# Second feed-forward product of a fp32 streaming layer by seven block products in two of three token blocks, with other token blocks

## The chip, the cores and the metric

One core of a Trainium2 chip runs the whole program. The metric is the device time of that core for one execution, in microseconds; lower is better. The names of the engines: PE multiplies matrices, DVE and POOL work element by element, ACT applies functions and copies, SP issues the DMAs. PEld is the loading of weights into PE, which goes on beside the matmuls.

## The reference, cut to what matters

A layer with a convolution mixer and a banded attention mixer, a gated merge of the two, and a gated feed-forward part. It runs on 2048 prompt tokens and 64 sample tokens; all weights and data are float32. The width D is 1024, the hidden width of the feed-forward part is 2816 (22 rows of 128).

```
merged = jax.nn.sigmoid(g_conv) * conv_out + jax.nn.sigmoid(g_attn) * attn_out
x = x + gt1 * (merged @ p['w_o'])

h2 = rms_norm(x, p['norm2_g']) * (1 + sc2) + sh2
gate, up = jnp.split(h2 @ p['w_ffn_in'], 2, axis=-1)
x = x + gt2 * ((jax.nn.silu(gate) * up) @ p['w_ffn_out'])
```

The change concerns the last line: the product of the hidden values, tokens x 2816, with `w_ffn_out`, 2816 x 1024.

## The kernel before, in words

**Numbers.** Every float32 operand of a product is split into a high part and a low part (the value minus the high part), both of a type that PE takes at its faster rate. One product is then three matmuls into the same PSUM bank: high by high, high by low, low by high (`mm3`, L613). For data ACT writes the high part and DVE subtracts the low one; for weights ACT writes the high part and POOL or DVE the low one.

**Stages.** The projections and the mixers run first, over four blocks of tokens (`PBLOCKS`, L35). They end near 1250 to 1360 us and the diff doesn't touch them. Then come the blocks of `CBLOCKS` (L36): tokens 0 to 704, 704 to 1344, 1344 to 2112. For each block the kernel does the gated merge (`merge`, L1512), the product with `w_o` (`wo`, L1661), the residual with norm and transposed columns (`residual`, L1539), and then the feed-forward part.

**The first feed-forward product** already goes by seven products for eight (`up`, L1743). Tokens are split into two halves of the block, D into two halves, and gate and up columns of one row f take the place of the two columns of a 2x2 block matrix. A row costs 7 x 4 x 3 = 84 matmuls whose moving width is half a block. It runs through the 22 rows in order. Its partial sums lie in PSUM banks of the tag "y" (four banks) and for one of them "gp" (four banks); ACT and DVE turn them into the hidden value of the row: tanh on ACT (`tg`), the gate's product on DVE, the factor, then the high part on ACT and the low part on DVE (`hidden`, L1717). The second half's split is put off into the next row (`late`).

**The second feed-forward product** (`down`, L1794) is plain. Once for every two rows, between two steps of `up`, it takes the two rows' hidden values as stationary operands: for each tile of 128 tokens and each of two column halves of 512, two rows x three matmuls into a "gp" bank; then DVE adds the bank to the token tile's sum `acc` in SBUF (for the first two rows ACT copies). The last four rows are done after all of `up`: there DVE adds `acc`, multiplies by the gate `gt`, adds the residual `x`, and the result is stored.

**Weights.** The class `Weights` (L250) goes through the list that `weight_order` (L499) writes out. Raw weights land in staging buffers ("wst", "wup", "wfo"; `free_tag`, L322; `load`, L329); `split` (L395) makes a slab of high and low parts, of which five are held; `done` gives one back. The seven products of `up` need sums of weight columns, which POOL makes (`operand`, L364; buffers `ws`) and which are kept in DRAM as `sum_d`. Keys of the kinds in `KEPT` (L60), the rows of `w_ffn_out` ("fo") among them, are stored in DRAM as high and low parts in the first block and read back in the later ones. Which engine subtracts is chosen at L426.

**What sets the order.** Instructions of PE stand as the code calls them. Everything else passes the planner (`Stream`, L159, and `Lane`, L106): it keeps a cost model of each engine's load, and lets side work in (weight slabs, residual steps, stores) where it reckons an engine free. All engine instructions are recorded at one line of a wrapper (L101), so the profile tells them apart by tiles: `ps` and `pd` are banks of the first and the second product, `t..` and `b..` the columns' operands, `whi`/`wlo` slabs, `hid` the hidden value's parts.

```
if j == 0 and 2 <= f <= NF - 4:
    yield from (("fo", f - 2), ("fo", f - 1))
```

## Time and profile before

| what | value |
| --- | --- |
| runs, us | 3053.41, 3048.85, 3043.31 |
| median, us | 3048.85 |
| profiled execution, span | 3049.1 us (no other time of it is given) |
| instructions | 44460 |
| HBM read, written | 501.70 MB, 171.61 MB |

The profile is one execution. Its page gives for each engine the busy time and the share of the span; the chain of waits follows the last instruction back to what released each step; a view by stretches gives busy time between two times; a view of groups gives for each operation and tile its count, the busy time in us, the mean of one in ns, and the idle time of the engine before it with what ended that. In the timeline a row has its start, its length, the engine, the line, the operation and the tiles; "x2" is two of a kind in a run, and a bracket names a wait that ended just before. A start less an earlier start of the same kind, divided by the matmuls between, is the cadence at which PE issues.

### The profile page before, as it was taken

How to read it: one execution, taken by the hardware profiler on the slowest of the kernel's cores; microseconds unless marked ns; L12 is line 12 of the kernel's file. 1: busy time of each engine (PE TensorE's matmuls, PEld its weight loads, DVE VectorE, ACT ScalarE, POOL GpSimd, SP SyncE). 2: the span in 40 equal slices, each digit the busy share in tenths (PEclk: the TensorE clock that was granted, in tenths of full speed). 3: DMA queues.
4: the chain of work that ended last, by engine and by line, in shares of the span. 5: the costliest groups of instructions: out<-in, count | busy, mean ns of one | idle time of the engine just before them, and what ended most of it. 6: DMA issues, size and time to landing. Idle time of an engine off the chain costs nothing.

```text
span 3049.1 us, 44460 instructions
## 1 busy us (share of the span) xinstructions
PE 2959.9 (97%) x16403; PEld 2633.0 (86%) x16403; DVE 1783.9 (59%) x3435; ACT 1180.2 (39%) x2110; POOL 1031.4 (34%) x642
## 2 busy tenths in 40 slices
PE   7989898999999999998999999999999999999999
PEld 4789776888888788898999998989999999999998
DVE  5797687867977895454443436554444556343345
ACT  3324531453255257355334343443333244322321
POOL 0200210101011102348778774344445343333431
PEclk9999998999999999999999999999999999999999
DMA  9888788888987788866455469754444965334434
GB/s 343 265 276 293 230 289 264 280 259 264 306 281 245 248 267 284 262 231 232 167 182 182 147 207 333 243 166 152 152 152 138 347 209 194 125 114 131 139 112 161
DMA packets 480167, 676.27 MB, mean 222 GB/s; under 512 B 37716, under 2 KB 316104, under 8 KB 479949
## 3 DMA queue, kind: packets, MB, share of 16 engines
q1 hardware_dynamic: 467669, 656.04, 65.7%
q10 hardware_dynamic: 12280, 17.39, 1.6%
q8 instruction: 129, 2.11, 0.3%
q14 instruction: 89, 0.73, 0.1%
HBM read 501.70 MB, written 171.61 MB: 221 GB/s over the span
## 4 chain that ended last, share of the span: by engine, by line
PE 83%; DVE 8%; DMA 4%; POOL 2%; issue 1%; ACT 1%; SPq 0%; ACTq 0%; POOLq 0%; DVEq 0%
PE ps L101 52%; PE pd L101 17%; PE pw L101 6%; DVE y L101 3%; PE po L101 2%; PE sc L101 2%; PE ptp L101 2%; POOL r L101 1%; PE pt L101 1%; PE pa L101 1%; DVE pr L101 1%; POOL wlo L101 1%; DMA whi<-w_dfi_h 0%; DMA kk<-k_d 0%; DMA wst<-in_w_in 0%
## 5 line engine op out<-in xcount | busy, mean ns | idle before, releaser
L101 POOL TENSOR_TENSOR wlo<-wst,whi 128x1024 fp32r<-128x1024 f32 (+1 forms) x213 | 452.1, 2132 | 586.4 <-ACT whi L101 465.5
L101 PE MATMUL ps<-t,whi 128*128 128x352 f32 (+2 forms) x2112 | 509.7, 324 | 10.7 <-ACT t L101 5.7
L101 PE MATMUL pd<-whi,hid 128*128 128x512 f32 (+1 forms) x1496 | 466.0, 389 | 0.0
L101 ACT ACTIVATE whi<-wst 128x1024 fp32r<-128x1024 f32 (+1 forms) x270 | 260.3, 973 | 448.0 <-PE pd L101 179.2
L101 PE MATMUL ps<-b,whi 128*128 128x352 f32 (+2 forms) x1584 | 382.1, 325 | 2.7 <-ACT early L101 1.9
L101 PEld LDWEIGHTS ps<-t,whi 128*128 128x128 f32 x2112 | 370.5, 189 | 16.1 <-ACT t L101 7.1
L101 DVE SCALAR_TENSOR_TENSOR y<-u,wd,y 128x512 f32<-128x512 f32 (+1 forms) x480 | 368.3, 771 | 6.5
L101 PE MATMUL ps<-hh,whi 128*128 128x512 f32 (+2 forms) x992 | 363.9, 367 | 0.0
L101 PE MATMUL ps<-hl,whi 128*128 128x512 f32 (+2 forms) x992 | 346.8, 350 | 0.0
L101 PE MATMUL ps<-hh,wlo 128*128 128x512 f32 (+2 forms) x992 | 346.4, 349 | 0.0
L101 PE MATMUL ps<-t,wlo 128*128 128x352 f32 (+2 forms) x1056 | 341.4, 323 | 0.1
L101 PEld LDWEIGHTS pd<-whi,hid 128*128 128x128 f32 (+1 forms) x1496 | 276.1, 185 | 62.5
L101 DVE TENSOR_TENSOR acc<-acc,pd 128x512 f32<-128x512 f32 (+1 forms) x272 | 186.9, 687 | 207.7 <-PE pd L101 206.8
L101 PE MATMUL pd<-wlo,hid 128*128 128x512 f32 (+1 forms) x748 | 291.6, 390 | 0.0
L101 PEld LDWEIGHTS ps<-b,whi 128*128 128x128 f32 x1584 | 276.9, 188 | 4.5 <-ACT early L101 2.8
L101 PE MATMUL ps<-b,wlo 128*128 128x352 f32 (+2 forms) x792 | 256.5, 324 | 0.0
L101 POOL TENSOR_TENSOR r<-t,mhalf 128x8 f32<-128x8 f32 (+3 forms) x68 | 84.8, 1249 | 401.0 <-DVE t L101 377.7
L101 POOL TENSOR_TENSOR wlo<-wup,whi 128x1024 fp32r<-128x1024 f32 (+1 forms) x73 | 158.9, 2177 | 171.1 <-ACT whi L101 171.1
L101 PEld LDWEIGHTS ps<-hh,wlo 128*128 128x128 f32 x992 | 188.1, 190 | 22.5
L101 PEld LDWEIGHTS ps<-hh,whi 128*128 128x128 f32 x992 | 189.0, 190 | 18.6 <-issue 2.1
L101 PEld LDWEIGHTS ps<-hl,whi 128*128 128x128 f32 x992 | 189.0, 191 | 15.4 <-issue 1.7
L101 PEld LDWEIGHTS ps<-t,wlo 128*128 128x128 f32 x1056 | 199.9, 189 | 0.4 <-POOL wlo L101 0.4
(206 smaller groups left out, 5431.0 us busy)
## 6 DMA issues: line engine op xcount, KB each, us to landing
whi<-w_din_h SPq DMA_DIRECT2D x72, 512.0 KB, 6.0
wlo<-w_din_l SPq DMA_DIRECT2D x72, 512.0 KB, 6.8
wst<-sum_d SPq DMA_DIRECT2D x133, 256.0 KB, 3.0
wmod<-in_w_ada SPq DMA_DIRECT2D x48, 512.0 KB, 8.6
sum_d<-ws SPq DMA_DIRECT2D x88, 256.0 KB, 4.6
whi<-w_dfo_h SPq DMA_DIRECT2D x44, 512.0 KB, 5.4
wlo<-w_dfo_l SPq DMA_DIRECT2D x44, 512.0 KB, 6.0
wst<-in_w_ffn_in SPq DMA_DIRECT2D x83, 256.0 KB, 3.4
```

What stands on the lines that cost most here:

```text
L101: return f(*args, **kw)
```

## The change

Blocks become tokens 0 to 576, 576 to 1344 and 1344 to 2112. In the last two blocks (`s` is 1 or 2) rows 4 to 19 of the second product go in pairs (`PAIRS`), e and o, by seven products for eight. The left matrix has the two halves of the block's tokens (i = 0, 1) as its rows and the hidden rows e and o as its columns; the right one has w rows e and o as its rows and the two halves of the 1024 columns as its columns. With A11, A21 the two halves of row e, and A12, A22 those of row o, DVE makes S3 = A11 - A21, S2 = A22 - S3, S1 = S2 + A11, S4 = A12 - S2 and each is split into high and low parts (`paired`, `put`). With B11, B12 the column halves of weight row e and B21, B22 those of row o, POOL makes T3 = B22 - B12, T1 = B12 - B11, T2 = B22 - T1, T4 = B21 - T2 in the second block (`down_parts`); the slabs are stored and read back in the third.

The seven products come in four slabs (`DN`) at four places of the next pair's `up` (`dn_at`): B21 and T3 before the s1 step of the even row, T4 and B11 before its a22 step, T2 and T1, then B22, in the odd row (for the last pair B22 after all of `up`). Each product is three groups of three matmuls of 512 columns, one for every 128 tokens of a half. T4 goes on in the banks of T3, and T2, T1 and B22 in those of B11 (`CHAIN`); after each product DVE adds the bank as it then stands to one of the four quarters of `acc` (`INTO`), so that a bank is read between two of its partial sums. Only rows 20 and 21 are left for the last stage of these blocks. Before the first block's third and fourth row and for all its rows `down` stays as it was; rows 4 to 19 are not stored there any more, and their raw rows are loaded again in the second block (items "fr").

Further: where the planner's POOL load is more than 4 us ahead of PE's (`BEHIND`), the low parts of weights go to DVE; `tile_chunks` rounds up; buffers "t2" and "tg1" go from two to three; `hid` has eight slots of half a block in each of these blocks.

```
-CBLOCKS = [(0, 704), (704, 1344), (1344, 2112)]
+CBLOCKS = [(0, 576), (576, 1344), (1344, 2112)]
-KEPT = ("qkv", "in", "fi", "fo")
+KEPT = ("qkv", "in", "fi", "fo", "dn")
+PAIRS = range(4, NF - 2, 2)
+DN = (("B21", "T3"), ("T4", "B11"), ("T2", "T1"), ("B22",))
+BEHIND = 4000.0
...
-    t, n = tiles[len(tiles) // 2 - 1]
+    t, n = tiles[(len(tiles) + 1) // 2 - 1]
...
+        if name == "pool" and self.sum_pool and self.stream.load["pool"] - self.stream.load["pe"] > BEHIND:
+            e, name = self.dve, "dve"
...
+        elif key[0] == "dn":
+            parts = [(slice(j, j + 1), part) for j, part in enumerate(self.down_parts(key))]
             self.stream.after("act", "pool")
...
+def dn_at(f):
+    return (0, 1, 3, 6 if f == PAIRS[-1] else 4)
...
-                if j == 0 and 2 <= f <= NF - 4:
+                if s and f - 2 in PAIRS:
+                    if j // 2 in dn_at(f - 2):
+                        yield ("dn", f - 2, dn_at(f - 2).index(j // 2))
+                elif j == 0 and 2 <= f <= NF - 4:
                     yield from (("fo", f - 2), ("fo", f - 1))
-        yield from (("fo", f) for f in range(NF - 4, NF))
+        yield from (("fo", f) for f in range(NF - 2 if s else NF - 4, NF))
...
+        def put(f, name, src):
+            q = quad[f - f % 2]
+            a = q["parts"][name] = slot(7 * (f // 2 - PAIRS.start // 2) + 4 + len(q["parts"]))
+            stream.after("act", "dve")
+            act.activation(a[:, 0], src, AF.Copy)
+            low(a[:, 0], a[:, 1], src, half)
...
+        LEFT = {"B21": "A12", "T3": "S3", "T4": "A22", "B11": "A11", "T2": "S2", "T1": "S1", "B22": "S4"}
+        INTO = {"B21": (0, 0), "T3": (1, 1), "T4": (1, 0), "B11": (0, 0), "T2": (1, 0), "T1": (1, 1), "B22": (0, 1)}
+        CHAIN = {"T4": "T3", "T2": "B11", "T1": "B11", "B22": "B11"}
+        def down_pair(f, j):
+            w = W.get(("dn", f, j))
+            for x, name in enumerate(DN[j]):
+                a = quad[f]["parts"][LEFT[name]]
+                for i in range(half // P):
+                    c = slice(P * i, P * i + P)
+                    key = CHAIN.get(name, name), i
+                    if name not in CHAIN:
+                        banks[key] = ps_g.tile([P, 512], F32, tag="gp", name="pd", bufs=4)
+                    ps = banks[key]
+                    mm3(ps, a[:, 0, c], a[:, 1, c], w[0][:, x], w[1][:, x], name not in CHAIN, True, skip_group_check=True)
+                    r, h = INTO[name]
+                    dst = acc[i + r * (half // P)][:, 512 * h : 512 * h + 512]
+                    stream.after("dve", "pe")
+                    dve.tensor_tensor(dst, dst, ps, ALU.add)
+            W.done()
...
-            up(f, ops, lambda: down([f - 2, f - 1], [W.get(("fo", e)) for e in (f - 2, f - 1)]) if 2 <= f <= NF - 4 else None)
-            up(f + 1, ops, lambda: None)
+            def at(i, f=f):
+                if s and f - 2 in PAIRS:
+                    if i in dn_at(f - 2):
+                        down_pair(f - 2, dn_at(f - 2).index(i))
+                elif i == 0 and 2 <= f <= NF - 4:
+                    down([f - 2, f - 1], [W.get(("fo", e)) for e in (f - 2, f - 1)])
+            up(f, ops, at)
+            up(f + 1, ops, at)
...
-        ws = [W.get(("fo", f)) for f in range(NF - 4, NF)]
+        end = NF - 2 if s else NF - 4
+        ws = [W.get(("fo", f)) for f in range(end, NF)]
```

The order of instructions, at three places. A number behind a name tells one buffer's use from another's.

Place 1, PE and DVE, a pair's second product in the third block. PE before: two rows (whi_28036, whi_28068) into one bank, then the next bank of the same tile.

```order
L101 MATMUL pd_28171<-whi_28036,hid_25172 128x512
L101 MATMUL pd_28171<-wlo_28037,hid_25172 128x512
L101 MATMUL pd_28171<-whi_28036,hid_25172 128x512
L101 MATMUL pd_28171<-whi_28068,hid_25172 128x512
L101 MATMUL pd_28171<-wlo_28069,hid_25172 128x512
L101 MATMUL pd_28171<-whi_28068,hid_25172 128x512
L101 MATMUL pd_28172<-whi_28036,hid_25172 128x512
```

PE of the change, the piece T4, B11, from its first matmul:

```order
L104 MATMUL pd_27093<-whi_26997,hid_26285 128x512
L104 MATMUL pd_27093<-wlo_26998,hid_26285 128x512
L104 MATMUL pd_27093<-whi_26997,hid_26285 128x512
L104 MATMUL pd_27098<-whi_26997,hid_26285 128x512
L104 MATMUL pd_27098<-wlo_26998,hid_26285 128x512
L104 MATMUL pd_27098<-whi_26997,hid_26285 128x512
L104 MATMUL pd_27103<-whi_26997,hid_26285 128x512
L104 MATMUL pd_27103<-wlo_26998,hid_26285 128x512
L104 MATMUL pd_27103<-whi_26997,hid_26285 128x512
L104 MATMUL pd_27161<-whi_26997,hid_25522 128x512
L104 MATMUL pd_27161<-wlo_26998,hid_25522 128x512
L104 MATMUL pd_27161<-whi_26997,hid_25522 128x512
```

and DVE of the change over the same piece:

```order
L104 TENSOR_TENSOR ps_27128<-ps_27128,s1_27007 128x384
L104 TENSOR_TENSOR acc_26084<-acc_26084,pd_27093 128x512
L104 SCALAR_TENSOR_TENSOR s1_27007<-tg_27142,ps_27128 128x384
L104 TENSOR_TENSOR acc_26101<-acc_26101,pd_27098 128x512
L104 TENSOR_TENSOR acc_26118<-acc_26118,pd_27103 128x512
L104 TENSOR_TENSOR acc_26020<-acc_26020,pd_27161 128x512
L104 TENSOR_TENSOR acc_26044<-acc_26044,pd_27166 128x512
L104 TENSOR_TENSOR acc_26061<-acc_26061,pd_27171 128x512
```

A group of three matmuls now fills a bank where six did, the banks of T4 (pd_27093 to pd_27103) were T3's before, and the gate's product stands between the first and the second read.

Place 2, ACT of the change at the same piece.

```order
L104 ACTIVATE hid_25522<-s1_26826 128x384
L104 ACTIVATE whi_27148<-wup_26936 128x1024
L104 ACTIVATE tg_27142<-ps_27128 128x384
L104 ACTIVATE hid_25522<-s1_27007 128x384
L104 ACTIVATE whi_27220<-wst_26994 128x1024
```

One weight slab's high part stands ahead of the tanh that the gate's product waits for. On DVE in the second block, at the opening piece of a pair (B21, T3), a slab's low part stands between the first and the second read:

```order
L104 TENSOR_TENSOR acc_20133<-acc_20133,pd_22076 128x512
L104 TENSOR_TENSOR wlo_22081<-wup_21888,whi_22080 128x1024
L104 TENSOR_TENSOR hid_20398<-s1_21803,hid_20398 128x384
L104 TENSOR_TENSOR acc_20157<-acc_20157,pd_22085 128x512
```

Before, that low part was POOL's.

Place 3, PE, one bank of a tile in the last stage. Before, four rows:

```order
L101 MATMUL pd_29158<-whi_28987,hid_28502 128x512
L101 MATMUL pd_29158<-wlo_28988,hid_28502 128x512
L101 MATMUL pd_29158<-whi_28987,hid_28502 128x512
L101 MATMUL pd_29158<-whi_29024,hid_28502 128x512
L101 MATMUL pd_29158<-wlo_29025,hid_28502 128x512
L101 MATMUL pd_29158<-whi_29024,hid_28502 128x512
L101 MATMUL pd_29158<-whi_29056,hid_25172 128x512
L101 MATMUL pd_29158<-wlo_29057,hid_25172 128x512
L101 MATMUL pd_29158<-whi_29056,hid_25172 128x512
L101 MATMUL pd_29158<-whi_29092,hid_25172 128x512
L101 MATMUL pd_29158<-wlo_29093,hid_25172 128x512
L101 MATMUL pd_29158<-whi_29092,hid_25172 128x512
```

and in the change two:

```order
L104 MATMUL pd_29712<-whi_29582,hid_26285 128x512
L104 MATMUL pd_29712<-wlo_29583,hid_26285 128x512
L104 MATMUL pd_29712<-whi_29582,hid_26285 128x512
L104 MATMUL pd_29712<-whi_29614,hid_26285 128x512
L104 MATMUL pd_29712<-wlo_29615,hid_26285 128x512
L104 MATMUL pd_29712<-whi_29614,hid_26285 128x512
L104 MATMUL pd_29713<-whi_29582,hid_26285 128x512
```

A bank is full after 6 matmuls instead of 12; DVE's operations on a tile are the same six.

More of the change, by code (lines that the diff above doesn't have):

```diff
@@ L269, in item @@
             return len(self.items) - 1
+        self.rows = {}
         for i, key in enumerate(keys):
             n = times[key] = times.get(key, 0) + 1
-            if key[0] == "up" and n == 1:
+            if key[0] == "dn" and n == 1:
+                for f in (key[1], key[1] + 1):
+                    if f not in self.rows:
+                        self.rows[f] = item(("fr", f))
+                self.need[i] = [self.rows[f] for f in (key[1], key[1] + 1)]
+                for j in self.rows_of(key):
+                    self.users[j] += 1
+            elif key[0] == "up" and n == 1:
                 self.first.add(i)
@@ L1639, in streaming_layer @@
             else:
-                turns.drain(groups[0])
+                turns.drain([gen for gen, (t, n) in zip(groups[0], tiles) if t - lo + n <= half])
             grp = [(t, n) for t, n in tiles if c0 <= t < c1]
@@ L1682, in streaming_layer @@
                 turns.add(gens[i])
-        hid = [wk.tile([P, 2, 2, CW], F32R, tag="m0", name="hid"), None]
+        hid = [wk.tile([P, 2, 2, CW] if not s else [P, 4, 2, CW // 2], F32R, tag="m0", name="hid"), None]
         early = wk.tile([P, 2 * EARLY - 2, CW // 2], F32, tag="m1", name="early")
@@ L1741, in streaming_layer, with rest_of_late, up @@
         begun, late = {}, []
-        def up(f, ops, between):
+        banks = {}
+        LEFT = {"B21": "A12", "T3": "S3", "T4": "A22", "B11": "A11", "T2": "S2", "T1": "S1", "B22": "S4"}
[17 more added lines that the diff above has]
+            W.done()
+        def rest_of_late(n=99):
+            while late and n:
+                n -= 1
+                if next(late[0], None) is None:
+                    late.pop(0)
+        def up(f, ops, at):
             def step(ps, op, b, first, last, e=f):
@@ L1759, in up @@
             step(y, "s2", "t2", f < EARLY, False)
-            if late:
-                hidden(*late.pop())
+            rest_of_late(1)
             u2 = piece("t1", "u2")[:, :half]
@@ L1777, in up @@
                 silu(c1, x)
+            if f % 2 == 0:
+                at(1)
             step(z, "a22", "t4", False, True)
             plus(z, z, u2)
-            dve.tensor_tensor(z, z, c1, ALU.mult)
+            two = s and f - f % 2 in PAIRS
+            h = [c1, v] if two else [z, y]
+            dve.tensor_tensor(h[0], z, c1, ALU.mult)
             if EARLY <= f + 1 < NF:
@@ L1785, in up @@
                 copy(begun[f + 1][1], ny)
-            hidden(f, 0, z)
+            for _ in paired(f, 0, h[0]) if two else [hidden(f, 0, z)]:
+                pass
             step(y, "s4", "b22", False, True)
@@ L1790, in up @@
             silu(y, y)
-            dve.tensor_tensor(y, y, v, ALU.mult)
-            late.append((f, 1, y))
+            dve.tensor_tensor(h[1], y, v, ALU.mult)
+            late.append(paired(f, 1, h[1]) if two else plain(f, 1, y))
         def down(fs, ws):
```

108 lines of the change are left out of this document (95 added, 13 removed).

## The prediction

> **What bounds the kernel now.** I read the page's head first, then its chain of waits, then busy time by stretches.
>
> ```profile
> span 3049.1 us, 44460 instructions
> PE 2959.9 (97%) x16403; PEld 2633.0 (86%) x16403; DVE 1783.9 (59%) x3435; ACT 1180.2 (39%) x2110; POOL 1031.4 (34%) x642
> PE 83%; DVE 8%; DMA 4%; POOL 2%; issue 1%; ACT 1%; SPq 0%; ACTq 0%; POOLq 0%; DVEq 0%
> ```
>
> PE is busy for 97% of the span and carries 83% of the chain. What the change touches lies after about 1360 us, and there the windows say more:
>
> ```profile
> core 0: us, PE busy (x) PEld busy (x) DVE busy (x) ACT busy (x) POOL busy (x), PEclk, DMA share, GB/s
> 1360.00:1410.00 50.00, 41.24 (x224) 37.79 (x223) 32.69 (x61) 32.09 (x68) 44.80 (x36) 0.93 0.77 265
> 1410.00:1800.00 390.00, 390.00 (x2154) 358.86 (x2154) 157.30 (x271) 146.35 (x275) 294.10 (x218) 1.00 0.52 172
> 1950.00:2000.00 50.00, 45.50 (x256) 40.24 (x255) 32.14 (x63) 28.22 (x56) 13.52 (x8) 1.00 0.71 241
> 2000.00:2350.00 350.00, 350.00 (x2083) 328.75 (x2082) 144.62 (x265) 121.03 (x194) 153.08 (x65) 1.00 0.46 149
> 2500.00:2560.00 60.00, 59.79 (x306) 53.35 (x305) 36.67 (x63) 30.63 (x55) 11.77 (x8) 1.00 0.57 193
> 2560.00:3010.00 450.00, 449.89 (x2380) 423.90 (x2379) 183.29 (x307) 141.26 (x219) 168.03 (x71) 1.00 0.40 128
> ```
>
> In the three feed-forward stretches (1410, 2000, 2560) PE never stops. A matmul taken out there is worth its whole cadence; a wait put in there costs its whole length. The rows at 1360, 1950 and 2500, the ways into these stretches, idle for 8.8, 4.5 and 0.2 us, in blocks whose half is 352, 320 and 384 tokens wide.
>
> **The change part by part.** First the price of three matmuls (one product of a row, hi and lo), as the distance between two records of the timeline:
>
> ```profile
> 170.63 0.29 PE L101 MATMUL ps<-hh,wlo 128*128 128x288 f32 x1
> 171.81 0.29 PE L101 MATMUL ps<-hh,wlo 128*128 128x288 f32 x1
> 1602.22 0.48 PE L101 MATMUL ps<-t,whi 128*128 128x352 f32 x2
> 1603.67 0.48 PE L101 MATMUL ps<-t,whi 128*128 128x352 f32 x2
> 2801.36 0.51 PE L101 MATMUL ps<-t,whi 128*128 128x384 f32 x2
> 2805.00 0.51 PE L101 MATMUL ps<-t,whi 128*128 128x384 f32 x2
> 2202.66 0.62 PE L101 MATMUL pd<-whi,hid 128*128 128x512 f32 x2
> 2205.39 0.62 PE L101 MATMUL pd<-whi,hid 128*128 128x512 f32 x2
> ```
>
> Between the pairs stand 9 matmuls of 288 columns, 9 of 352, 21 of 384 and 12 of 512: 0.393, 0.483, 0.52 and 0.68 us for three, so 0.2275 us for one of 512.
>
> *Matmuls taken out.* In a block of 768 tokens the 16 rows cost 6 tiles x 2 halves x 16 x 3 = 576 matmuls, by seven products 8 pairs x 7 x 3 tiles x 3 = 504. Before, the same holds for 2112 tokens in all, and the order has 16171 rows on PE before and 16027 after: 144 fewer. 144 x 0.2275 = **-32.8 us**.
>
> *Other block widths.* The halves become 288, 384 and 384 wide; before they were 352, 320 and 384, the same sum of 1056, and the cadence is nearly a straight line in the width (0.00136, 0.00137, 0.00135 us a column). **0**, with 3 us to both sides, 0.005 us on each of some 600 groups of three in the first product.
>
> *Reads between partial sums.* Each of the seven products is now added to the sums by DVE in three reads of a bank. How long a read and its neighbours take:
>
> ```profile
> L101 DVE TENSOR_TENSOR acc<-acc,pd 128x512 f32<-128x512 f32 x256 | 176.0, 687 | 187.7 <-PE pd L101 187.7
> L101 ACT ACTIVATE whi<-wst 128x1024 fp32r<-128x1024 f32 x216 | 227.7, 1060 | 421.0 <-PE pd L101 179.2 <-PE ps L101 90.4 <-issue 34.9
> L101 ACT ACTIVATE tg<-ps 128x384 f32<-128x384 f32 x44 | 21.4, 486 | 46.7 <-DVE ps L101 39.3 <-PE ps L101 7.4
> L101 DVE SCALAR_TENSOR_TENSOR ps<-tg,ps 128x384 f32<-128x384 f32 x54 | 30.3, 561 | 68.1 <-ACT tg L101 49.6 <-PE ps L101 18.4
> L101 ACT ACTIVATE hid<-ps 128x384 fp32r<-128x384 f32 x44 | 21.6, 492 | 53.2 <-DVE ps L101 53.2
> L101 DVE TENSOR_TENSOR hid<-ps,hid 128x384 fp32r<-128x384 f32 x44 | 24.5, 558 | 22.8 <-ACT hid L101 22.5
> L101 POOL TENSOR_TENSOR wlo<-ws,whi 128x512 fp32r<-128x512 f32 x88 | 113.8, 1302 | 83.5 <-ACT whi L101 83.1 <-PE pd L101 0.3
> L101 DVE TENSOR_TENSOR wlo<-wst,whi 128x1024 fp32r<-128x1024 f32 x57 | 73.5, 1292 | 60.0 <-ACT whi L101 59.4 <-issue 0.4
> ```
>
> and how late one engine answers the other, in the timeline and in the chain of waits:
>
> ```profile
> 1601.99 0.39 PE L101 MATMUL pd<-whi,hid 128*128 128x512 f32 x1
> 1602.42 0.69 DVE L101 TENSOR_TENSOR acc<-acc,pd 128x512 f32<-128x512 f32 x1 [0.67 <-PE pd L101]
> 1403.19 0.70 DVE t L101
> 1403.93 17.89 PE ps L101 x95
> ```
>
> The read starts 0.20 us after the next matmul could issue (1602.22 above), and PE goes on 0.04 after DVE ends (1403.19 + 0.70 to 1403.93). A group of three takes 0.68, its read 0.69, so PE and DVE are level as long as DVE does nothing else. The two middle pieces of a pair are three groups on held banks and then three more that need those banks. Count from the first matmul. The read of the first bank runs 0.88 to 1.57. Meanwhile ACT splits a weight slab that comes free at 0: 0.20 to 1.26, and after it the gate's tanh (or the hidden value's high part) 1.26 to 1.75; DVE, in order, takes the gate's product at 1.79 to 2.35 before the second read, which ends at 3.0. PE wants that bank after four groups, at 2.72, and has it at 3.04: 0.3 us. The third read, 3.0 to 3.7, is in time for 3.7. Two pieces, 16 pairs: 32 x 0.3 = **+9.6**. If ACT stands free DVE is ahead and it is 0 (from 2.72 the reads are covered); if a second slab stands on ACT it is 0.3 + 1.06 = 1.36 each, +43.5. I take 0.3 since the order shows one slab between them.
>
> "Perfetto Trace Analysis" in the Trainium skill ("Optimizing Tensor Performance", Matmuls) says that independent groups should go round different banks, so that emptying one overlaps the next one's matmuls. Here chained products return to a bank they left. Taken as a single bank, nine groups of each pair would stand for 0.20 + 0.69 + 0.04 = 0.93: 16 x 9 x 0.93 = 134 us, and the kernel would be at some 3160. The 0.3 rests on three banks in turn.
>
> *One split on DVE in the second block.* The order has one subtraction of 128x1024 between the first and second read of the opening piece. Third bank wanted after five groups plus 0.52, at 3.92; read done at 0.20 + 0.68 + 0.69 + 1.29 + 0.56 + 0.69 = 4.11. 0.2 x 8 = **+1.6** (none to 1.3 each, +10).
>
> *The last stage.* Two rows are left for it, formerly four. Its DVE work on a tile is six operations, in the end of the timeline:
>
> ```profile
> 3016.69 1.38 DVE L101 TENSOR_TENSOR pd<-pd,acc 128x512 f32<-128x512 f32 x2 [1.78 <-PE pd L101]
> 3017.98 1.29 DVE L101 TENSOR_TENSOR pd<-pd,gt 128x512 f32<-128x512 f32 x2
> 3019.18 1.27 DVE L101 TENSOR_TENSOR acc<-pd,x 128x512 f32<-128x512 f32 x2
> 3020.37 0.69 DVE L101 TENSOR_TENSOR pd<-pd,acc 128x512 f32<-128x512 f32 x1
> 3036.41 0.70 DVE L101 TENSOR_TENSOR pd<-pd,acc 128x512 f32<-128x512 f32 x1 [0.56 <-PE pd L101]
> 3039.13 0.70 DVE L101 TENSOR_TENSOR pd<-pd,acc 128x512 f32<-128x512 f32 x1 [0.56 <-PE pd L101]
> 3044.14 0.39 PE L101 MATMUL pd<-whi,hid 128*128 128x512 f32 x1
> 3045.31 0.69 DVE L101 TENSOR_TENSOR acc<-pd,acc 128x512 f32<-128x512 f32 x1
> ```
>
> 3016.69 to 3020.37: 3.68 us a tile. PE's 24 matmuls (two halves of 2.72 each, 3036.41 to 3039.13) were longer, and DVE waited. With 12 (2.73) DVE is the slower. From the last step of the first product on: the last pair's three groups are 2.04, the first tile's first bank is full at 2.04 + 9 x 0.2275 + 0.2 = 4.3, and from there five tiles are 18.4, then two preparing adds (1.2) and four last operations (2.6): 26.5. By PE alone it would be 2.04 + 6 x 2.73 + 0.2 + 1.4 (two operations, as after 3044.14) = 20.0. So **+6.5** at the end. In the second block the sixth tile's banks are the fourth's, which DVE leaves at 4.3 + 4 x 3.68 = 19.0 and PE wants at 2.0 + 5 x 2.73 = 15.7: **+3.3**. If the stage before it lets DVE start late, 2 us more at each.
>
> *The ways in.* The second block's half becomes 384 wide, and there the idle time was 0.2, not 4.5: -4.3. The first block's becomes narrower, so ten products of 12 matmuls that cover the columns are shorter by 10 x 12 x (0.483 - 0.393)/3 = 3.6; half of it exposed, +1.8. Together **-2.5** (0 to -4.3).
>
> *Priced at nothing.* POOL in the first block is busy for 294 of 390 us; with 576 tokens for 704 the stretch shrinks to 390 x 576/704 = 319, which would leave it no slack. About 90 subtractions, at 1.30 us and more each, go to DVE (157 of 390 there) under the new rule: at least 117 us off POOL, hidden. Should each of the 90 set DVE back by the 0.2 of the second block's, +18. POOL in the second block gets about 11 more operations of 1.30 us a pair, 14.3 us, together some 31 of 43.5, a share that stood beside PE at 390 of 390 in the first block. The slices stored and reread meet a DMA share of 0.40 to 0.46.
>
> Sum against the profiled span, for which no other time is given: 3049.1 - 32.8 + 9.6 + 1.6 + 9.8 - 2.5 = **3034.8**. The runs' median is 3048.85, the same within 0.3 us, so I predict **3035 us**, 0.45% less.
>
> **The rivals.** R1, *all reads covered*: ACT's slab comes late enough for DVE to keep ahead. For it: DVE and ACT are busy for under half of 2560 to 3010. Against it: both run in order. 3035 - 11.2 = 3024.
>
> R2, *a second slab on ACT*: at half of the 32 places one more convert of 1.06 stands ahead of the tanh. For it: the first product's slabs pass ACT throughout, and in the second block the new right-hand slabs too, four a pair, with five held. 16 x 1.06 = +17: 3052, no change.
>
> R3, *the granted clock drops after the gaps*: the row at 1360 granted 0.93, which is 3.5 us lost in 50, behind 8.8 us of idle time. Once in each pair, 16 x 3.5 = +56: 3091. Against it: the row at 1950 idled 4.5 us and kept 1.00. The Trainium skill's "TensorE: Matmul & The Clock Gate" ("A second HAM failure mode: psum-queue depth-cycling") tells of such re-throttling where banks are cycled; the row at 1950 does not bear it out.
>
> R4, *slower: the second block's slices come late from POOL*. It makes four sums a pair and their low parts, each 1.30, behind the first product's. If two of four slabs a pair come two low parts late, 8 x 2 x 2.6 = +42: 3077. It is slower than before from 14.3 + 9 = 23 us, 2.9 a pair. For it: sums depend on one another, T1 before T2 before T4, and the rows they take may load late. Against it: 71% busy leaves 12 us a pair.
>
> **How the numbers follow.** Forecast 0.42 (own range 3025 to 3042), R1 0.10, R2 0.20, R3 0.06, R4 0.22. About 0.3%, 9 us, is what a measurement of this kernel can tell from no change: 3039.7 to 3058.0 is the same. The forecast gives 0.40 to faster and 0.02 to same, R1 faster; of R2 0.18 is same and 0.02 slower; R3 and R4 are slower. Faster 0.50, same 0.20, slower 0.30. R1 at 3024 with its 3 us of widths and a last stage 3 us better is 3018; the upper end takes R4's middle, 3077, and leaves its upper half and R3 out.
>
> **What would show it.** In the windows of the last two feed-forward stretches PE should idle for 0.5 to 1 us a pair, each on a bank that DVE reads, none on a low part of a slab (that would be R4), with the clock at 1.00 (else R3). DVE's rows of acc<-acc,pd should count about 424 at 0.69. The end of the timeline should show DVE back to back through the last five tiles. Wrong is the sum if the last stage waits on anything else, or if the stretch of the first block shows PE idle beside POOL's or DVE's splits.

## The result, and the profile after

| kernel | median, us | runs |
| --- | --- | --- |
| before | 3047.68 | 4, 3043.31 to 3053.41 |
| changed | 3088.59 | 4, 3085.31 to 3091.31 |

The change makes the kernel slower: the ratio is 1.0129, with a 95% interval of 1.0109 to 1.0148, some 40 us. The forecast was 3035 with a range up to 3078.

The head of the page of the changed kernel, and then its busy time by stretches, cut at the same stages as before (the ways into a feed-forward part at 1350, 1925 and 2580, each followed by the part itself; the columns are those of the windows shown for the kernel before):

```profile
span 3089.5 us, 44838 instructions
PE 2948.6 (95%) x16259; PEld 2611.9 (85%) x16259; DVE 2092.8 (68%) x3817; ACT 1233.9 (40%) x2212; POOL 1005.2 (33%) x626
```

```profile
1350.00:1400.00 50.00, 38.14 (x247) 36.29 (x246) 34.31 (x63) 26.87 (x55) 28.97 (x22) 0.89 0.76 262
1400.00:1760.00 360.00, 355.22 (x2225) 322.10 (x2225) 239.93 (x367) 147.44 (x293) 220.33 (x149) 1.00 0.54 175
1925.00:1975.00 50.00, 47.63 (x253) 45.63 (x252) 34.41 (x54) 22.79 (x40) 7.79 (x3) 0.97 0.41 137
1975.00:2400.00 425.00, 407.17 (x2118) 376.39 (x2117) 263.28 (x401) 168.72 (x273) 263.30 (x149) 1.00 0.53 173
2580.00:2640.00 60.00, 57.59 (x301) 54.03 (x302) 36.52 (x58) 29.11 (x49) 7.82 (x4) 0.97 0.37 124
2640.00:3060.00 420.00, 407.79 (x2147) 381.92 (x2146) 257.43 (x404) 132.75 (x214) 162.64 (x72) 1.00 0.49 158
```

The 144 matmuls are gone, 16259 in place of 16403. But PE, which all but never stopped in these parts before, now stands for 4.8 us in the first, 17.8 in the second and 12.2 in the third. What it waits for in the second and in the third is one thing, in the view of waits (what waited, for what, us in total, how often, the longest), first of 1975 to 2400:

```profile
PE pd L104 <- DVE acc L104: 17.8, 18, 1.7
```

and of 2640 to 3060:

```profile
PE pd L104 <- DVE acc L104: 12.2, 7, 1.7
```

These are the reads between partial sums. In seven of the third block's eight pairs PE waits 1.7 us for one. In the second block there are 18 waits of several lengths. The timeline of one such place in the third block (start, length, engine, operation; a bracket names the wait before) shows why:

```profile
2725.44 0.69 DVE L104 TENSOR_TENSOR acc<-acc,pd 128x512 f32<-128x512 f32 x1 [0.51 <-PE pd L104]
2725.53 0.51 ACT L104 ACTIVATE hid<-v 128x384 fp32r<-128x384 f32 x1
2725.76 2.38 POOL L104 TENSOR_TENSOR wlo<-wst,whi 128x1024 fp32r<-128x1024 f32 x1 [1.79 <-ACT whi L104]
2726.07 2.48 DVE L104 TENSOR_TENSOR hid<-v,hid 128x384 fp32r<-128x384 f32 x1
2728.48 3.12 DVE L104 TENSOR_TENSOR acc<-acc,pd 128x512 f32<-128x512 f32 x5
2729.21 0.50 PE L104 MATMUL pd<-whi,hid 128*128 128x512 f32 x1 [1.74 <-DVE acc L104]
```

A subtraction of 128x384 on DVE, the low part of a hidden value, takes 2.48 us in place of 0.56. It starts while POOL subtracts a weight slab's low part (2725.76 to 2728.14) and ends 0.41 us after POOL does. The reads behind it on DVE are late by 1.9, and PE with them. In the kernel before, the hidden value lay in PSUM (`hid<-ps,hid`, 558 ns); now it lies in SBUF (`hid<-v,hid`), both inputs do, and here such an instruction of DVE stands still beside one of POOL. The runs below test that reading.

### The profile page after: what moved, and what is told of

Its sections match the earlier page's. It is cut to its first block, busy times and chain, and to the rows that moved or that the text cites. A ratio compares the mean times of both kernels' runs of the same rounds, so it can differ in the third digit from the quotient of the medians.

```text
span 3089.5 us, 44838 instructions
## 1 busy us (share of the span) xinstructions
PE 2948.6 (95%) x16259; PEld 2611.9 (85%) x16259; DVE 2092.8 (68%) x3817; ACT 1233.9 (40%) x2212; POOL 1005.2 (33%) x626
## 5 line engine op out<-in xcount | busy, mean ns | idle before, releaser
L104 POOL TENSOR_TENSOR wlo<-wst,whi 128x1024 fp32r<-128x1024 f32 (+1 forms) x175 | 391.6, 2244 | 485.6 <-ACT whi L104 421.5
L104 PE MATMUL ps<-t,whi 128*128 128x384 f32 (+1 forms) x2112 | 503.4, 324 | 11.0 <-DVE t L104 4.8
L104 PE MATMUL pd<-whi,hid 128*128 128x512 f32 (+1 forms) x1400 | 455.1, 394 | 33.4 <-DVE acc L104 33.4
L104 PE MATMUL ps<-b,whi 128*128 128x384 f32 (+1 forms) x1584 | 382.6, 327 | 10.8 <-DVE pw L104 4.0
L104 PEld LDWEIGHTS pd<-whi,hid 128*128 128x128 f32 (+1 forms) x1400 | 258.2, 184 | 104.3 <-DVE acc L104 47.0
L104 PE MATMUL ps<-t,wlo 128*128 128x384 f32 (+1 forms) x1056 | 340.6, 323 | 0.0
L104 DVE TENSOR_TENSOR acc<-acc,pd 128x512 f32<-128x512 f32 (+1 forms) x440 | 285.3, 681 | 66.4 <-PE pd L104 62.8
L104 PE MATMUL pd<-wlo,hid 128*128 128x512 f32 (+1 forms) x700 | 274.1, 392 | 0.0
L104 PE MATMUL ps<-b,wlo 128*128 128x384 f32 (+1 forms) x792 | 257.9, 326 | 0.0
L104 POOL TENSOR_TENSOR wlo<-wup,whi 128x1024 fp32r<-128x1024 f32 (+1 forms) x62 | 133.9, 2160 | 208.7 <-ACT whi L104 202.4
```

What stands on the lines that cost most here:

```text
L104: return f(*args, **kw)
```

## The experiments: what the blocks cost

**e1_blocks** is the kernel before with the new blocks alone.

```
-CBLOCKS = [(0, 704), (704, 1344), (1344, 2112)]
+CBLOCKS = [(0, 576), (576, 1344), (1344, 2112)]
-    t, n = tiles[len(tiles) // 2 - 1]
+    t, n = tiles[(len(tiles) + 1) // 2 - 1]
-                turns.drain(groups[0])
+                turns.drain([gen for gen, (t, n) in zip(groups[0], tiles) if t - lo + n <= half])
```

> The kernel before with the new blocks and what they need (chunks rounded up, the drained tiles), and nothing else: no seven products in the second product, no rule that moves low parts to DVE. Theory A (the loss is in the last two blocks' pairs and last stages): within 9 us of before, 3040 to 3057, with the first block's feed-forward stretch losing no more than the 15 us it loses before. Theory B (the blocks cost it: in the changed kernel the merges and the ways in lose some 15 us more than before): 3060 or more.

Measured: 3085.02 against 3049.07, ratio 1.0115 (1.0100 to 1.0130). My theory A fell: the blocks by themselves cost 36 us. The first block's part in its windows:

```profile
1400.00:1760.00 360.00, 347.62 (x2176) 316.35 (x2175) 143.97 (x275) 146.07 (x290) 310.15 (x228) 0.99 0.64 213
```

PE idles here for 12.4 us. POOL is busy for 310 of 360 us, and it works in bursts that are not spread as PE wants them. One of the waits, in the timeline:

```profile
1721.93 1.27 POOL L101 TENSOR_TENSOR ws<-wst 128x512 f32<-128x512 f32 x1
1722.01 0.63 ACT L101 ACTIVATE whi<-ws 128x512 fp32r<-128x512 f32 x1 [6.86 <-POOL ws L101]
1722.84 0.40 ACT L101 ACTIVATE s<-ps 128x288 f32<-128x288 f32 x1
1723.29 0.85 PE L101 MATMUL ps<-t,whi 128*128 128x288 f32 x2 [5.58 <-ACT s L101]
```

ACT, in order, stood 6.86 us before a weight sum that POOL had not made, and a copy out of PSUM stood behind it, for which PE waited 5.58. The view of waits puts that down to ACT (`s`); the cause is one step further. A second part of the loss lies behind this window, in the merge and the product with `w_o` of the second block, where PE waits for the high and low parts of weights (waits, 1760 to 1900; in the kernel before, the same stage has one wait of 0.2 us):

```profile
PE ps L101 <- ACT whi L101: 6.2, 3, 4.1
PE ps L101 <- POOL wlo L101: 4.3, 4, 1.5
```

**e9_behind** adds the rule for POOL.

```
+BEHIND = 4000.0
...
+        if name == "pool" and self.sum_pool and self.stream.load["pool"] - self.stream.load["pe"] > BEHIND:
+            e, name = self.dve, "dve"
```

> The kernel before with the new blocks (as in e1_blocks) and the rule that gives low parts to DVE when POOL is behind; still no seven products in the second product. Theory A: the 36 us of e1_blocks come from POOL, which has no slack left in the narrower first block (waits of PE of 3.7 and 5.7 us there, and of some 15 us in the merge behind it); the rule takes away about 15 of them, and the seven products cost the rest of the change's 40: 3063 to 3073 here. Theory B: the rule brings nothing, since DVE's subtractions then stand beside POOL's: 3080 or more, and the seven products would be worth nothing either way.

Measured: 3072.09 against 3048.20, ratio 1.0085 (1.0070 to 1.0100). The rule gives 13 us back, and 24 stay. In the window of the first block PE now idles for 4.8 us instead of 12.4; the longest waits that stay (4.0 and 3.6 us for DVE, 3.2 for ACT) lie outside it, in the ways in and the merge. What the rule moves to DVE has both inputs in SBUF. DVE's groups of the first block, 1400 to 1760, in the changed kernel, which has the same rule:

```profile
L104 DVE TENSOR_TENSOR wlo<-ws,whi 128x512 fp32r<-128x512 f32 x50 | 56.7, 1140 | 5.5 <-ACT whi L104 3.3
L104 DVE TENSOR_TENSOR wlo<-wst,whi 128x512 fp32r<-128x512 f32 x14 | 19.2, 1377 | 10.4 <-ACT whi L104 10.3
```

A mean of 1.14 and 1.38 us; with POOL idle the same 128x512 takes 0.69 (e12_sums, below). One place where this costs PE time is the way into the third block, here in the changed kernel; e9_behind has the same wait of 2.4 us, and e1_blocks, without the rule, has not:

```profile
2591.54 2.39 POOL L104 TENSOR_TENSOR wlo<-wst,whi 128x1024 fp32r<-128x1024 f32 x1 [14.88 <-ACT whi L104]
2592.41 2.61 DVE L104 TENSOR_TENSOR wlo<-wst,whi 128x1024 fp32r<-128x1024 f32 x1
2596.27 0.44 PE L104 MATMUL ps<-t,whi 128*128 128x384 f32 x1 [2.41 <-DVE t L104]
```

No run separates how much of the 24 us comes from such subtractions and how much from the load that stays with POOL.

**e14_cover** is e1_blocks without POOL's low parts from the first block's feed-forward part up to the second block's: zeros are written in their place, so the low parts of those weights are left out of the result, in the later blocks too where they are read back. (`W.third` is set anew only where the next feed-forward part begins, so the merge between them has the zeros too, 22 of 128x1024 from 1760 to 1950, which the expectation doesn't say.)

```
+            if self.third and name == "pool":
+                e.memset(lo[:, c].bitcast(F32), 0.0)
+                continue
             e.tensor_tensor(lo[:, c], src, hi[:, c].bitcast(F32), ALU.subtract)
...
+        W.third = s == 0
```

> e1_blocks, and in the first block's feed-forward part POOL writes zeros (0.96 us for 128x1024) in place of the weights' low parts (2.4 us), which are left out of the result; everything else, the sums on POOL, ACT's high parts, the loads and stores, stays. Theory A (POOL's work on the weights has too little to hide behind in a first block of 576 tokens): the 36 us that the blocks cost go, 3043 to 3056. Theory B (the blocks cost it by shorter cover for the columns, for ACT or for the DMAs): 3065 or more stays.

Measured: 3055.76 against 3052.00, ratio 1.0015 (1.0004 to 1.0026). The blocks' cost is gone but for 4 us: it was POOL's low parts of weights in the first block and in the merge behind it, some of them made once for all blocks, that have no room beside 576 tokens. A zero takes POOL less time, and it also spares the reading that the next section is about; but in e1_blocks' window every DVE instruction with two tensors for inputs has one of them in PSUM, so what the zeros free there is POOL's time. POOL in the same window (the fifth busy time):

```profile
1400.00:1760.00 360.00, 358.11 (x2246) 326.33 (x2245) 159.56 (x295) 143.38 (x283) 173.14 (x220) 1.00 0.66 222
```

## The experiments: what holds the reads

**e2_memset** is the change with zeros written by POOL in place of the weights' low parts in the third block; those are left out of the result. The edit is e14_cover's, with `s == 2`.

> The changed kernel; in the third block POOL writes zeros in place of the low parts of the weights (they are left out of the result) and so reads nothing from SBUF there; every instruction of DVE stays. Theory A (a DVE subtraction with both inputs in SBUF stands still while POOL works on SBUF: 2.48 us beside POOL, 0.56 without): those subtractions take 0.56, the seven waits of PE of 1.9 us in the third block's pairs shrink to 0.5 or less each, the kernel is 9 to 13 us shorter, some 3077. Theory B (DVE simply has too many operations at that place): the waits stay at 1.5 us or more and the time within 3 us of the change. Between them: if writing alone blocks as well, the subtractions still exceed 0.56 beside POOL.

Measured: 3067.44 against 3049.07, ratio 1.0057 (1.0037 to 1.0077), 21 us less than the change, where 9 to 13 were expected. The traces place the difference. Up to the third block both kernels run the same instructions, yet in the profiled executions the first matmul of the second product starts at 1405.64 in the change and at 1396.04 here:

```profile
1405.64 0.39 PE L104 MATMUL pd<-whi,hid 128*64 128x512 f32 x1
```

```profile
1396.04 0.40 PE L104 MATMUL pd<-whi,hid 128*64 128x512 f32 x1
```

So 9.6 us of the difference between these two executions are not the edit's. From the third block's first such matmul to its last the change takes 458.3 us and e2_memset 444.8: the edit is worth 13.5, a little more than the seven waits of 12.2. DVE's groups in the third block, first of the change, 2580 to 3060 (count, busy us, mean ns):

```profile
L104 DVE TENSOR_TENSOR hid<-v,hid 128x384 fp32r<-128x384 f32 x24 | 26.7, 1111 | 0.6 <-ACT hid L104 0.6
L104 DVE TENSOR_TENSOR hid<-s,hid 128x384 fp32r<-128x384 f32 x23 | 16.1, 702 | 8.9 <-ACT hid L104 8.9
```

then of e2_memset:

```profile
L104 DVE TENSOR_TENSOR hid<-v,hid 128x384 fp32r<-128x384 f32 x24 | 13.3, 556 | 0.6 <-ACT hid L104 0.6
L104 DVE TENSOR_TENSOR hid<-s,hid 128x384 fp32r<-128x384 f32 x23 | 12.8, 557 | 8.9 <-ACT hid L104 8.9
```

The same instructions in the same numbers take 556 ns. The zeros take POOL 0.96 us where a subtraction took 2.4, so POOL works less too. But writing alone doesn't hold DVE: in each pair of the third block DVE instructions with both inputs in SBUF fall beside a write, as far as the profile places POOL's (its spans on POOL are rough), and take 0.55 us all the same.

```profile
2737.72 0.55 DVE L104 TENSOR_TENSOR hid<-v,hid 128x384 fp32r<-128x384 f32 x1
2737.93 0.96 POOL L104 MEMSET wlo<- 128x1024 f32 x1 [3.20 <-PE ps L104]
2738.19 0.55 DVE L104 TENSOR_TENSOR s<-s,v 128x384 f32<-128x384 f32 x1
```

**e3_nopool** leaves nothing out: in the third block the weights' low parts, and all of the hidden values', are DVE's.

```
+        if name == "pool" and self.third or name == "pool" and self.sum_pool and ...
...
+            dve.tensor_tensor(a[:, 1], src, a[:, 0].bitcast(F32), ALU.subtract)
```

> The changed kernel; in the third block the low parts of the weights and of the hidden values are all DVE's, so that POOL is idle there. DVE gets some 70 more operations of 1.29 us, 90 us on 509, and loses its waits for POOL. Theory A: no subtraction with two SBUF inputs exceeds 0.56 (128x384) or 1.3 (128x1024) in the third block, and PE's waits move to where a 1.29 stands between two reads, up to 1 us a pair: time 3078 to 3088. Theory B (DVE's load decides): waits of 3 us or more in each pair, time over 3095.

Measured: 3071.85 against 3049.07, ratio 1.0072 (1.0051 to 1.0092): 17 us less than the change though DVE has some 70 operations more, and better than the 3078 to 3088 expected; no wait moved to the slabs' subtractions. PE's waits of 2640 to 3060 in all:

```profile
PE pd L104 <- DVE acc L104: 1.1, 2, 0.6
```

12.2 us became 1.1, and those two lie in the last stage. The rival, that DVE has too much to do there, falls: with more to do it is in time.

**e5_third** has the old blocks, and seven products in the third block alone (each test on `s` becomes `s == 2`, `BEHIND = 1e9`), where POOL then makes the slices too.

> The old blocks (704, 640, 768), seven products in the third block alone, made there, and no rule that moves low parts to DVE. Theory A (the pairs lose more than their matmuls save): the third block's feed-forward stretch, 504.7 us before, is not shorter by the 16.4 us of its 72 matmuls but longer, 505 to 530, since POOL's sums now fall into this block; time 3050 to 3075. Theory B (new blocks and moved low parts cost it, the pairs gain): 3040 or less.

Measured: 3061.36 against 3049.07, ratio 1.0037 (1.0025 to 1.0050). So the seven products lose by themselves, without the blocks, when they are made and used beside POOL.

**e7_dve23** is e3_nopool for both blocks (`W.third = s >= 1`); POOL keeps the four sums of a pair. **e7_mixed** leaves the right-hand slabs' low parts with POOL as well.

> The change with the low parts of the weights, the right-hand slabs' among them, and of the hidden values on DVE in the second and the third block; POOL keeps only the four sums of a pair in the second. Theory A (two SBUF inputs on DVE beside POOL): the second block's waits at reads, 24 us in the change, shrink to under 10 and the third block keeps the 15 us that e3_nopool gained: 3050 to 3064. Theory B (DVE, 332 of 517 us busy there and now given 100 us more, becomes the bound): the second block gets no shorter, 3070 or more.

> As e7_dve23, but the right-hand slabs' low parts stay with POOL in the second block (some 10 us of POOL a pair beside the sums). Theory A: longer than e7_dve23 by 2 to 8 us where DVE has room, since DVE's subtractions wait for POOL again. Theory B (DVE's load decides): shorter than e7_dve23.

Measured: 3057.76 (ratio 1.0035, 1.0021 to 1.0048) and 3068.36 (1.0070, 1.0050 to 1.0090) against 3048.20. Both are faster than the change, by 31 and by 20 us, e7_dve23 more, in which POOL does less; the distance between them, 10.6, is more than the 2 to 8 expected. What the sums still cost in e7_dve23's second block, 1975 to 2400, is in DVE's groups

```profile
L104 DVE TENSOR_TENSOR wlo<-wst,whi 128x1024 fp32r<-128x1024 f32 x46 | 61.7, 1343 | 23.3 <-ACT whi L104 23.3
```

and in the waits:

```profile
PE pd L104 <- DVE acc L104: 7.1, 7, 1.6
```

**e8_last** is e3_nopool with part of the last stage's work on POOL: on the last three tiles it prepares `acc` times the gate plus the residual, and DVE has four operations on each instead of six.

```
+                ready = last and s and i >= len(tiles) // 2
+                if ready:
+                    for j in range(2):
+                        dst = acc[i][:n, 512 * j : 512 * j + 512]
+                        stream.after("pool", "dve")
+                        gps.tensor_tensor(dst, dst, gt[:n, 512 * j : 512 * j + 512], ALU.mult)
+                        gps.tensor_tensor(dst, dst, x1[j], ALU.add)
```

> e3_nopool, and in the last stages of the second and third block POOL prepares the last three tiles (acc times the gate, plus the residual), so that DVE has four operations on each instead of six. Theory A (DVE, 3.68 us a tile against 2.73 of PE, sets the last stage): three tiles at 2.76, the end of the kernel is 2 to 4 us sooner, and the three waits of 0.7 us before the end vanish: 3066 to 3070 against 3072. Theory B (the end hangs on the stores or on POOL's own 1.3 us operations): no gain or a loss.

Measured: 3069.34 against 3048.20, ratio 1.0074 (1.0059 to 1.0089); against e3_nopool's 3071.85 the difference of 2.5 us has the size that was expected but is within the runs' spread. In the traces PE's last matmul starts 5.6 us before the end of the span instead of 8.3 in e3_nopool; of the three waits before the end two stay, 1.1 us together. The last stage of the changed kernel itself, in its timeline:

```profile
3074.25 1.28 DVE L104 TENSOR_TENSOR acc<-pd,x 128x512 f32<-128x512 f32 x2
3074.98 0.50 PE L104 MATMUL pd<-whi,hid 128*128 128x512 f32 x1 [0.53 <-DVE acc L104]
3075.45 1.29 DVE L104 TENSOR_TENSOR pd<-pd,acc 128x512 f32<-128x512 f32 x2
...
3077.84 1.27 DVE L104 TENSOR_TENSOR acc<-pd,x 128x512 f32<-128x512 f32 x2
3078.57 0.50 PE L104 MATMUL pd<-whi,hid 128*128 128x512 f32 x1 [0.56 <-DVE acc L104]
...
3081.21 0.39 PE L104 MATMUL pd<-whi,hid 128*128 128x512 f32 x1
```

A tile every 3.59 us (3074.98 to 3078.57), with DVE back to back and PE waiting for each.

## The experiments: towards a version that gains

**e10_third** is e5_third with e3_nopool's and e8_last's edits. **e11_made** makes the slices in the second block instead, beside its plain product, and reads them back in the third.

```
+MAKE = {1: (0,), 3: (1,), 4: (2, 3)}
...
+                elif s == 1 and f - 2 in PAIRS and i in MAKE:
+                    for k in MAKE[i]:
+                        W.get(("dn", f - 2, k))
+                        W.done()
```

> e5_third (old blocks, seven products in the third block alone, slices made there) with the low parts of weights and hidden values on DVE in the third block and the last three tiles prepared by POOL. Theory A: e5_third's waits of some 1.1 to 1.9 us in each pair mostly go, as in the second block of e7_dve23 (504 us with slices made beside it, 1.0 left in each pair), and the end is 3 us sooner: 3044 to 3054 against e5_third's 3061. Theory B (the rest is DVE's load): 3056 or more.

> e10_third with the slices made in the second block, beside its plain product, by POOL (four sums and seven low parts a pair), stored, and read back in the third. Theory A: the third block's feed-forward stretch is 493 us, as in e3_nopool, against 503 before, the second's stays at 431 within 4 us, since DVE has few operations with two SBUF inputs there; 3036 to 3044, faster than the kernel before. Theory B (the second block pays for the making): its stretch is 10 us longer or more, and the time is not under 3046.

Measured: 3059.76 (ratio 1.0025, 1.0014 to 1.0037) and 3082.67 (1.0109, 1.0088 to 1.0129) against 3053.28. Both are slower than the kernel before and missed what was expected. In e11_made the second block pays, mostly in one wait at its end (waits, 1970 to 2480):

```profile
PE pd L105 <- DMA wlo<-w_dfo_l: 26.2, 2, 24.2
```

The rows of the last stage are read back too late; by the order of the list, the slices of the last pair stand before them among the five slabs held, but that this is the reason wasn't tried. In e10_third PE's waits at reads are hardly less than in e5_third (12.3 us against 13.0): one of about 1.6 us is left in seven of the eight pairs, and the timeline shows what stands there:

```profile
2738.53 3.15 POOL L104 TENSOR_TENSOR ws<-wfo,ws 128x512 f32<-128x512 f32 x2
2740.43 2.33 DVE L104 TENSOR_TENSOR wlo<-wup,whi 128x1024 fp32r<-128x1024 f32 x1
2742.68 3.12 DVE L104 TENSOR_TENSOR acc<-acc,pd 128x512 f32<-128x512 f32 x5
2743.41 0.50 PE L104 MATMUL pd<-whi,hid 128*128 128x512 f32 x1 [1.64 <-DVE acc L104]
```

It is POOL's sums (to 2741.68) that hold DVE's subtraction now.

**e12_sums** puts these four sums on DVE; **e13_all** does the same with the new blocks, on e7_dve23, with e8_last's edit. (With the sums on DVE the loader has to take the raw rows for a slab of kind "dn" from its own list.)

```
-                self.gps.tensor_tensor(t, x, y, ALU.subtract)
+                (self.dve if self.third else self.gps).tensor_tensor(t, x, y, ALU.subtract)
-        return "fo" if key[0] in ("fo", "fr") else ""
+        return "fo" if key[0] in ("fo", "fr", "dn") else ""
```

> e10_third with the four sums of a pair on DVE too, so that POOL is idle in the third block's feed-forward part until the last stage. Theory A (what is left of the waits, 1.8 us in each pair, is DVE's subtraction of a slab that stands beside POOL's sums, 2.33 us in place of 1.23): the waits fall under 0.8, though DVE gets 2.8 us a pair more; 3046 to 3054 where the kernel before has 3050. Theory B (DVE, 417 of 506 us busy there, is full): the waits stay or grow, 3058 or more.

> e7_dve23 with the sums on DVE and the last three tiles of the last stages prepared by POOL. Theory A: e7_dve23's seven waits of 1.0 to 1.8 us in the second block fall under 0.5, the end is 3 us sooner: 3045 to 3054 against its 3058. Theory B (DVE is full): 3058 or more.

Measured: **3044.97** against 3050.52, ratio 0.9983 (0.9972 to 0.9993), and 3056.52, ratio 1.0022 (1.0011 to 1.0033). e12_sums is the one version here that beats both kernels, by 5 us against the one before, a little under the range expected. e13_all lies between its two expectations. e12_sums' third block in the windows, DVE's groups from 2580 to 3060, and all waits on DVE's reads of 1340 to 3060:

```profile
2554.00:3030.00 476.00, 473.54 (x2483) 441.54 (x2483) 399.85 (x637) 192.02 (x318) 15.09 (x12) 1.00 0.36 113
```

```profile
L104 DVE TENSOR_TENSOR wlo<-wst,whi 128x1024 fp32r<-128x1024 f32 x48 | 58.6, 1222 | 30.9 <-ACT whi L104 30.9
L104 DVE TENSOR_TENSOR wlo<-ws,whi 128x512 fp32r<-128x512 f32 x32 | 21.4, 687 | 2.9 <-ACT whi L104 2.9
L104 DVE TENSOR_TENSOR hid<-v,hid 128x384 fp32r<-128x384 f32 x24 | 13.3, 555 | 0.6 <-ACT hid L104 0.6
```

```profile
PE pd L104 <- DVE acc L104: 1.1, 2, 0.6
```

DVE is busy for 84% of that stretch (400 of 476 us) and still in time for the reads, with nothing of POOL's beside it in the pairs (its 15 us are the last stage's). The two waits that are left lie in the last stage. e13_all shows the same for the second block, where the change's waits were the most, 17.8 us; from 1965 to 2390 its view of waits has no row, and the window is

```profile
1975.00:2400.00 425.00, 423.75 (x2212) 393.85 (x2211) 369.38 (x590) 164.90 (x271) 15.06 (x12) 1.00 0.59 197
```

So what held the reads of the pairs is POOL's work beside DVE's, in both blocks. e13_all keeps its first block's cost: it is 12 us slower than e12_sums.

## Why the prediction was wrong, point by point

**Direction and sum.** The change costs 41 us by the medians in place of a gain of 14. By e9_behind, which has all of it but the seven products, the blocks and the rule cost 3072.1 - 3048.2 = 24, and the seven products 3088.6 - 3072.1 = 16.5, where the forecast had -2.5 (the ways in) and -32.8 + 9.6 + 1.6 + 9.8 = -11.8. R3's 3091 is near the measured time by chance alone, since the drop of the clock on which it rests isn't there.

With what was measured below, the seven products' terms give -32.8 + 30 + 7 = 4, so some 12 of their 16.5 us are in none of them. The stretches from the first to the last matmul of the second product say where to look: in the second and the third block they are 457.5 and 456.8 us in e9_behind, 467.1 and 458.3 in the change, and 445.1 and 444.7 in e13_all. POOL's work beside the pairs thus goes with 22 and 13.6 us of the change (some 1 us of each is e8_last's edit), more than the waits of 17.8 and 12.2; and without it the 72 matmuls fewer of a block shorten its stretch by 12 us, not by 72 x 0.2275 = 16.4. The reason for that is open.

**Matmuls taken out, -32.8.** Right in count (144 fewer) and nearly in the price of one: groups that wait for nothing stand 0.68 to 0.69 us apart.

**Reads between partial sums, +9.6 + 1.6.** This step failed: the reads were the right place for a loss, but its cause and its size were not. I took 0.3 us for each of two places in a pair from the order of DVE's and ACT's instructions, and the durations from rows of the kernel before. The waits were 17.8 + 12.2 = 30 us. One of the durations did not hold in the changed kernel: 558 ns was that of a subtraction with one input in PSUM, and the change puts that value into SBUF. The row for such an instruction with both inputs in SBUF stood in the prediction, `wlo<-wst,whi` on DVE at 1292 ns, and I read it as a plain duration; undisturbed it is 1222. The second converted slab on ACT, rival R2, was not what held the reads either: with POOL idle, e12_sums and e3_nopool have no such wait, which is better than my 0.3. The waits of neither R3 nor R4 are there: the clock is 1.00 in both long stretches, and no wait on a slab's low part stands among those of the second block.

**Priced at nothing.** The second step that failed, and the larger one: POOL's work in the narrower first block. I saw that a stretch of 319 us would leave no slack for POOL's 294 and let the new rule hide it at DVE. The blocks alone cost 36 us, of which the rule took back 13 (e1_blocks, e9_behind), and what it moved is the same kind of subtraction; without POOL's low parts the cost is 4 us (e14_cover). The bound of +18 stood in the working, but only for DVE set back by 0.2 each, and the number taken was 0.

**The ways in, -2.5.** The second block's idle time did fall, from 4.5 to 2.4 us, though not to 0.2; the first one's rose from 8.8 to 11.9, with the clock at 0.89 against 0.93, and the third one's from 0.2 to 2.4. Together +3.2. For the first block I had left 1.8 of 3.6 us of lost cover exposed, and the row says 3.1; that all of it is this cover was not tried. The third block's 2.4 us was in none of my terms and is the rule's: one wait behind a low part that DVE subtracts beside POOL, in 2.61 us for 1.22 (shown with e9_behind). The second block's 2.4 us is a wait of the same kind. In e1_blocks, which has the blocks without the rule, the second way in idles for 0.3 us, as forecast.

**The last stage, +9.8.** The mechanism was right, DVE paces it with 3.59 us a tile (3.68 forecast), and the size roughly: PE's last matmul starts 8.3 us before the end of the span, 5.0 before the change (3081.21 of 3089.5 and 3044.14 of 3049.1), 3.3 more. In the third block PE's tiles, 12 matmuls or 2.73 us each, come 3.59 apart, and PE stands for 0.5 to 0.6 before three of them, 1.7 us in all; the view of waits has the same 1.7 in the second block's last stage. Together some 7.

**Other block widths, 0.** With POOL's low parts out of the way, e14_cover is within 4 us of the kernel before.

## What to carry to other kernels

When a change moves a value from PSUM to SBUF, or a subtraction from POOL to DVE, look up where each input of the DVE instruction lies: with both in SBUF its duration depends on what POOL does at that time, and the sum has to be made with the disturbed one wherever DVE's next instruction is waited for. Work that is done once for all blocks, here POOL's sums and part of its splitting of weights, is covered mainly by the first block; a narrower first block must be priced against that engine's busy time, in bursts and not on the mean. And an engine that is only 33% busy can be the cause of waits (here 30 us at the reads) that name another engine: the test is to silence it. Taking only part of its work away can leave the waits as they were (e10_third).

## What the runs showed of the hardware

A DVE TENSOR_TENSOR with both inputs in SBUF took up to 2.48 us beside a POOL subtraction, for 0.56 alone (128x384), and 2.61 for 1.22 (128x1024); beside a POOL write of zeros it took 0.55 (e2_memset); with one input in PSUM nothing of the kind showed (`hid<-ps,hid` has a mean of 558 ns beside a POOL that is busy for a third of the time). In the timeline at 2726.07 it begins after POOL's has begun and ends after POOL's has ended. The Trainium skill has this in "SBUF — State Buffer", section "Who interferes with whom": a DVE instruction with two SBUF inputs contends with one of GpSimd that reads SBUF, and whichever comes first keeps the other out. The runs agree with it where they show it, the undisturbed rows beside zeros included. Not expected was how far it reaches: 30 us of PE's time at the reads, through an engine that had 2% of the chain of waits in the kernel before.
